# A decoder step whose MLP's first product is made of seven block products for eight, with its activations through DRAM

## The chip, the cores and the metric

The program runs on one core of one Trainium2 chip. The metric is device time in microseconds (us), the median of several runs. A profiled execution gives the trace that all rows below come from.

## The reference, cut to what matters

One step of a decoder layer for 1024 prompt tokens and 32 new tokens (8 sequences of 4), 1056 columns of tokens in all. Attention, a short convolution and their merge come first and are not touched. The change is in the last part:

```
def merge_and_mlp(x, a, c, ga, gb, w_nsa_out, w_conv_out, w_o, g_mlp, w_up, w_down):
    m = jax.nn.sigmoid(ga) * (a @ w_nsa_out) + jax.nn.sigmoid(gb) * (c @ w_conv_out)
    x = x + m @ w_o
    h = rms_norm(x, g_mlp)
    return x + jnp.square(jax.nn.relu(h @ w_up)) @ w_down
```

`h` is 1056 tokens by 1024 features, `w_up` is 1024 x 4096, `w_down` 4096 x 1024, all float32. A final RMSNorm follows.

## The kernel before, in words

Every float32 product is made of three matmuls: an operand is split into a high part (a cast to the type `F32R`) and a low part (what is left), and `mm3` (lines 211 to 214) adds high by high, high by low and low by high. So each line of a product shows up three times in the profile, as L212, L213 and L214. The high part of a weight is cast on ACT, its low part subtracted on POOL (`wsplit`, lines 228 to 236, and `load_down`, lines 1414 to 1424).

**w_o** (lines 1329 to 1359) runs over two halves of 512 output columns, and in each over nine tiles of tokens (eight of 128, one of 32), tokens in rows. In the second half each tile is added to the residual, stored to DRAM (`x2_d`), normalised (ACT squares, POOL takes the root, DVE scales) and transposed on TensorE (`transpose_split`, lines 199 to 209) into `h2h` and `h2l`, high and low parts with features in rows: 8 tiles k of 128 features by 1056 tokens.

**The MLP** (lines 1386 to 1430) goes in eight blocks of four tiles of 128 features of the 4096. In a block the up products come first: for each of the four tiles, three PSUM banks of 384, 384 and 288 token columns (`BANKS`), each summed over 8 k; then ACT's relu, DVE's square, ACT's cast and DVE's low part give `uh` and `ul`, in five buffers. Then the down products of the block: for each of 8 tiles of output features and each of the three banks, four k by three matmuls, added on DVE to `acc`. The up products of the first two tiles (`NU0 = 2`, lines 1361 to 1376) use room that w_o leaves and stand ahead of the blocks:

```
            for c0, c1 in BANKS:
                s = slice(c0, c1)
                po = gemm_T(wu, (h2h, h2l), KT, c0, c1, "up") if f0 >= NU0 * 128 else po0.pop(0)
                r = lp.tile([128, 384], F32, name="r", tag="r")[:, :c1 - c0]
                S.activation(r, po, AF.Relu)
                V.tensor_mul(r, r, r)
                S.copy(uh[:, s], r)
                V.tensor_sub(ul[:, s], r, f32(uh[:, s]))
```

**The end** (from line 1432): the last block's down products come in two groups of columns (`LASTB`, 640 to 1056 and 256 to 640), with the transposes back, the residual and the final norm of each group's tokens behind it; the first 256 tokens come last, with tokens in rows.

**The order of work.** The program says what is done on which engine. Each engine takes its instructions in one order, which a planner sets for the whole program by simulated times; so an engine's order need not be that of the lines. All loads and stores but the gathers are issued by SP, in one queue. A pool of SBUF or PSUM that opens where another closed waits, tile by tile, for the readers of what lay there.

## Time and profile before

| | us |
|---|---|
| median of 3 runs | 2036.77 |
| the runs | 2036.88, 2036.77, 2031.64 |
| the profiled execution, first to last instruction (span) | 2030.1 |
| TensorE busy in it | 1995.6 |
| DVE, ACT, POOL busy | 885.3, 684.3, 602.8 |

Of the profiled execution the trace has the span alone; between it and the median lie 6.7 us. Busy times are sums over the span; a matmul's duration in the trace includes its way through the array, so consecutive matmuls overlap, and what a matmul costs in a row of them is the distance of the starts. PE is TensorE's matmuls, PEld its weight loads, DVE VectorE, ACT ScalarE, POOL GpSimd, SP the engine that issues DMAs.

### The profile page before, as it was taken

How to read it: one execution, taken by the hardware profiler on the slowest of the kernel's cores; microseconds unless marked ns; L12 is line 12 of the kernel's file. 1: busy time of each engine (PE TensorE's matmuls, PEld its weight loads, DVE VectorE, ACT ScalarE, POOL GpSimd, SP SyncE). 2: the span in 40 equal slices, each digit the busy share in tenths (PEclk: the TensorE clock that was granted, in tenths of full speed). 3: DMA queues.
4: the chain of work that ended last, by engine and by line, in shares of the span. 5: the costliest groups of instructions: out<-in, count | busy, mean ns of one | idle time of the engine just before them, and what ended most of it. 6: DMA issues, size and time to landing. Idle time of an engine off the chain costs nothing.

```text
span 2030.1 us, 32304 instructions
## 1 busy us (share of the span) xinstructions
PE 1995.6 (98%) x12644; PEld 1865.3 (92%) x12644; DVE 885.3 (44%) x1930; ACT 684.3 (34%) x1606; POOL 602.8 (30%) x725
## 2 busy tenths in 40 slices
PE   9999999999999999899999899999999999999998
PEld 7999999999998898778788888999999999999998
DVE  5323242445447666464432624534242333333334
ACT  5113224555556566343221303413121222213123
POOL 3121223443344444432332501422122212221203
PEclk9999999999999999999999999999999999999999
DMA  6365226222247311564453534311111111111113
GB/s 209 125 158 132 83 63 168 71 67 65 67 121 246 127 50 48 176 205 156 139 158 132 185 126 139 105 53 42 42 52 42 49 46 47 37 53 41 42 65 117
DMA packets 215463, 205.67 MB, mean 101 GB/s; under 512 B 16213, under 2 KB 185318, under 8 KB 213264
## 3 DMA queue, kind: packets, MB, share of 16 engines
q1 hardware_dynamic: 208400, 170.06, 28.0%
q0 software_dynamic: 6912, 33.56, 4.9%
q8 instruction: 99, 1.62, 0.3%
q14 instruction: 52, 0.43, 0.1%
HBM read 158.95 MB, written 44.63 MB: 100 GB/s over the span
## 4 chain that ended last, share of the span: by engine, by line
PE 78%; DMA 2%; DVE 1%; ACT 1%; issue 0%; POOL 0%; SPq 0%; DVEq 0%; POOLq 0%; ACTq 0%
PE up L214 6%; PE up L212 6%; PE up L213 6%; PE dn L212 6%; PE dn L213 6%; PE dn L214 6%; PE PT L874 3%; PE hid L212 3%; PE ga L213 3%; PE hid L213 3%; PE ga L212 3%; PE ga L214 3%; PE hid L214 3%; PE pv L881 2%; PE pv L880 2%; PE sl L1127 2%
## 5 line engine op out<-in xcount | busy, mean ns | idle before, releaser
L235 POOL TENSOR_TENSOR wlu<-wru,whu 128x1024 fp32r<-128x1024 f32 x62 | 149.3, 2409 | 483.4 <-ACT whu L234 483.4
L213 PE MATMUL dn<-ul,whd 128*128 128x384 f32 (+2 forms) x736 | 239.1, 325 | 0.0
L214 PE MATMUL dn<-uh,wld 128*128 128x384 f32 (+2 forms) x736 | 239.1, 325 | 0.0
L212 PE MATMUL dn<-uh,whd 128*128 128x384 f32 (+2 forms) x736 | 238.3, 326 | 0.0
L212 PE MATMUL up<-h2h,whu 128*128 128x384 f32 (+1 forms) x720 | 232.9, 323 | 0.0
L214 PE MATMUL up<-h2h,wlu 128*128 128x384 f32 x720 | 232.8, 324 | 0.0
L213 PE MATMUL up<-h2l,whu 128*128 128x384 f32 (+1 forms) x720 | 232.5, 323 | 0.0
L800 POOL TENSOR_SCALAR P<-P,st,gates 128x256 f32<-128x256 f32 (+4 forms) x272 | 150.7, 571 | 123.1 <-DVE st L796 94.3
L1400 DVE TENSOR_TENSOR r<-r 128x384 f32<-128x384 f32 (+1 forms) x96 | 108.2, 1128 | 180.2 <-ACT r L1399 178.3
L1412 DVE TENSOR_TENSOR acc<-dn,acc 128x384 f32<-128x384 f32 (+1 forms) x160 | 84.3, 528 | 195.1 <-PE dn L214 195.1
L1423 POOL TENSOR_TENSOR wld<-wrd,whd 128x512 fp32r<-128x512 f32 x64 | 83.8, 1311 | 248.4 <-ACT whd L1422 248.4
L212 PE MATMUL hid<-cth,w1h 128*128 128x254 f32 x512 | 148.5, 290 | 5.7 <-ACT cth L509 5.6
L213 PE MATMUL hid<-ctl,w1h 128*128 128x254 f32 x512 | 149.6, 292 | 0.0
L214 PE MATMUL hid<-cth,w1l 128*128 128x254 f32 x512 | 145.7, 285 | 0.0
L214 PEld LDWEIGHTS dn<-uh,wld 128*128 128x128 f32 x736 | 138.4, 188 | 0.0
L213 PEld LDWEIGHTS dn<-ul,whd 128*128 128x128 f32 x736 | 138.4, 188 | 0.0
L212 PEld LDWEIGHTS dn<-uh,whd 128*128 128x128 f32 x736 | 137.9, 188 | 0.1
L213 PEld LDWEIGHTS up<-h2l,whu 128*128 128x128 f32 x720 | 135.8, 189 | 0.0
L212 PEld LDWEIGHTS up<-h2h,whu 128*128 128x128 f32 x720 | 135.4, 188 | 0.0
L214 PEld LDWEIGHTS up<-h2h,wlu 128*128 128x128 f32 x720 | 135.3, 188 | 0.0
L1422 ACT CAST whd<-wrd 128x512 fp32r<-128x512 f32 x64 | 39.8, 621 | 265.3 <-PE dn L213 263.6
L212 PE MATMUL ga<-hTh,whu 128*128 128x384 f32 (+1 forms) x384 | 127.8, 333 | 0.0
(410 smaller groups left out, 4927.0 us busy)
## 6 DMA issues: line engine op xcount, KB each, us to landing
wru<-in_w_in SPq DMA_DIRECT2D x32, 512.0 KB
wrd<-in_w_down SPq DMA_DIRECT2D x64, 256.0 KB
wru<-in_w_up SPq DMA_DIRECT2D x30, 512.0 KB
tb<-tb_d SPq DMA_DIRECT2D x8, 528.0 KB
cg_d<-tb SPq DMA_DIRECT2D x8, 528.0 KB
ta<-ta_d SPq DMA_DIRECT2D x8, 528.0 KB
cg<-cg_d SPq DMA_DIRECT2D x8, 528.0 KB
w1r<-in_cmp_w_k SPq DMA_DIRECT2D x16, 256.0 KB
```

Of the source, the lines that this page charges most:

```text
L212: PE.matmul(out, wh, ah, start=first, stop=False)
L213: PE.matmul(out, wh, al, start=False, stop=False)
L214: PE.matmul(out, wl, ah, start=False, stop=last)
L235: (leng or P.tensor_sub)(l, raw, f32(h))
L800: P.tensor_scalar(p, p, self.st[:, br, 3, g:g + 1], gates[:, self.qi, 3 * hg + br:3 * hg + br + 1], op0=OP.mult, op1=OP.mult)
L874: PE.transpose(pt[:n, g * 128:(g + 1) * 128], pg[g], ident)
L880: PE.matmul(self.o, w, hi[:n], start=first and i == 0, stop=False)
L881: PE.matmul(self.o, w, lo[:n], start=False, stop=last and i == len(tiles) - 1)
L1127: PE.matmul(pl[l][rows[j], :], qb[b], kt, start=True, stop=True)
L1400: V.tensor_mul(r, r, r)
L1412: V.tensor_add(acc[:, j, s], po, acc[:, j, s])
L1423: P.tensor_sub(l, raw, f32(h))
```

## The change

The 1024 features of `h` are taken as two halves, the 1056 tokens as two halves of 528 (each with 512 prompt tokens and 16 new ones, which changes the order of the columns), and the 4096 features of the MLP as 16 pairs of tiles (p and p + 16). Of such a 2 x 2 x 2 product, seven block products of [512 x 128] by [512 x 528] are made for eight, from sums and differences of the blocks of `w_up` (s1 to s4, on DVE, anew for each pair) and of `h` (t1 to t4, once, on POOL and DVE); sums of the products give the four results. The operands that are made of `h` are split into high and low parts in a stage after w_o; the first block product's two operands (`hA`) are split tile by tile as before. In w_o's second half the 32 new tokens come fifth, not last. `relu(x)` times `x` is one DVE operation; its result is stored to DRAM (`u_d`) and loaded again by the down products, which become a stage of their own and keep their blocks of four. PSUM is four double banks during the up products. The last block's groups of columns are 264, 264 and 272 wide.

```diff
+HC = T // 2
...
-NU0 = 2
...
-LASTB = [(640, T), (256, 640)]
+LASTB = [(HC, HC + 264, (4, 5)), (HC + 264, T, (6, 7)), (256, HC, (2, 3, 8))]
+TORDER = [(0, 1, 2, 3, 4, 5, 6, 7, 8), (0, 1, 2, 3, 8, 4, 5, 6, 7)]
+NP0 = 2
+WUB = 7
...
+    u_d = dr.tile([32, 128, 2, HC], F32, name="u_d")
...
     h2p = open_pool("h2", "left")
-    h2h = h2p.tile([128, KT, T], F32R, name="h2h")
-    h2l = h2p.tile([128, KT, T], F32R, name="h2l")
+    hA = [[h2p.tile([128, 4, HC], F32R, name=f"hA{q}{x}") for x in "hl"] for q in range(2)]
+    h2r = [[[h2p.tile([128, HC], F32, name="h2r", tag="h2r", bufs=16) for _ in range(4)] for _ in range(2)] for _ in range(2)]
+    (r11, r12), (r21, r22) = h2r
     fp = open_pool("F", "left", bufs=2)
     g2 = fp.tile([128, D], F32, name="g2", bufs=1)
     DMA.dma_start(g2, g_mlp.to_broadcast([128, D]))
+    def columns(tt):
+        if tt < 8:
+            return [(tt // 4, slice(tt % 4 * 128, tt % 4 * 128 + 128), slice(0, 128))]
+        return [(h, slice(512, HC), slice(16 * h, 16 * h + 16)) for h in range(2)]
+    def transpose_h2(xn, m, tt):
+        for q in range(2):
+            pt = ps("tp", "xT")
+            pv = pt.rearrange("p (k t) -> p k t", k=4)
+            for i in range(4):
+                k = 4 * q + i
+                PE.transpose(pv[:, i, :m], xn[:m, k * 128:(k + 1) * 128], ident[:m, :m])
+            for half, c, s in columns(tt):
+                for k in range(4):
+                    S.copy(h2r[q][half][k][:, c], pv[:, k, s])
+                if half == 0:
+                    h = hA[q][0][:, :, c]
+                    V.tensor_copy(h, pv[:, :, s])
+                    V.tensor_sub(hA[q][1][:, :, c], pv[:, :, s], f32(h))
+        c = columns(tt)[-1][1]
+        if tt >= 4:
+            for k in range(4):
+                P.tensor_sub(r11[k][:, c], r12[k][:, c], r11[k][:, c])
+                P.tensor_sub(r12[k][:, c], r22[k][:, c], r12[k][:, c])
     for half in range(2):
         hs = slice(half * 512, half * 512 + 512)
         if half:
             wo = load_wo(1)
-        for tt in range(9):
+        for tt in TORDER[half]:
...
-                transpose_split(xn, m, h2h, h2l, tt * 128)
-    po0 = []
-    for j in range(NU0):
-        wu0 = []
+                transpose_h2(xn, m, tt)
+    early_w = []
+    for p in range(NP0):
         for q in range(2):
             raw, h, l = (wop.tile([128, 512], dt, name="wo" + n, tag="wo" + n, bufs=b).rearrange("p (k c) -> p k c", k=4)
                          for n, dt, b in (("r", F32, 2), ("h", F32R, WOB), ("l", F32R, WOB)))
-            DMA.dma_start(raw, w_up[0, q * 512:(q + 1) * 512, j * 128:(j + 1) * 128].rearrange("(k p) c -> p k c", p=128))
+            DMA.dma_start(raw, w_up[0, q * 512:(q + 1) * 512, p * 128:(p + 1) * 128].rearrange("(k p) c -> p k c", p=128))
             S.copy(h, raw)
             V.tensor_sub(l, raw, f32(h))
-            wu0 += [(h[:, k], l[:, k]) for k in range(4)]
-        for c0, c1 in BANKS:
-            po = ps("gx", "up")[:, :c1 - c0]
-            for k in range(KT):
-                mm3(po, *wu0[k], h2h[:, k, c0:c1], h2l[:, k, c0:c1], k == 0, k == KT - 1)
-            po0.append(po)
-    close("F", "wo", "m")
+            early_w.append((h, l))
+    open_psum(c=4)
+    def product(w, h):
+        c = bank["p"].tile([128, 2, 512], F32, name="c", tag="c", bufs=4)[:, :, :HC // 2]
+        for k in range(4):
+            for i in range(2):
+                s = slice(i * HC // 2, (i + 1) * HC // 2)
+                low = h[1][k] if isinstance(h[1], list) else h[1][:, k]
+                mm3(c[:, i], w[0][:, k], w[1][:, k], h[0][:, k, s], low[:, s], k == 0, k == 3)
+        return c
+    close("F")
+    qp = open_pool("q", "left")
+    def part(tag, bufs=1):
+        return qp.tile([128, 2, HC // 2], F32, name=tag, tag=tag, bufs=bufs)
+    def first_two(w11, w12):
+        p1 = part("p1", NP0)
+        S.copy(p1, product(w11, hA[0]))
+        x = part("x", 3)
+        V.tensor_add(x, product(w12, hA[1]), p1)
+        return p1, x
+    begun = [first_two(*early_w[2 * p:2 * p + 2]) for p in range(NP0)]
+    close("wo", "m")
+    hbp = open_pool("hB", "right")
+    t2 = [hbp.tile([128, HC], F32, name="t2", tag="t2", bufs=4) for _ in range(4)]
+    for k in range(4):
+        V.tensor_sub(t2[k], r22[k], r11[k])
+        V.tensor_sub(r21[k], r21[k], t2[k])
+    hB = {}
+    for n, raw, low, pool, tag in (("t2", t2, V, hbp, "l2"), ("t3", r12, P, hbp, "t2"), ("t1", r11, V, h2p, "h2r"),
+                                   ("t4", r21, P, h2p, "h2r"), ("b22", r22, V, h2p, "h2r")):
+        h = hbp.tile([128, 4, HC], F32R, name="hB" + n)
+        l = [pool.tile([128, HC], F32R, name=tag, tag=tag, bufs=16 if tag == "h2r" else 4) for _ in range(4)]
+        for k in range(4):
+            S.copy(h[:, k], raw[k])
+            low.tensor_sub(l[k], raw[k], f32(h[:, k]))
+        hB[n] = (h, l)
+    wp = open_pool("w", "right", bufs=2)
+    def halves(raw):
+        h, l = (wp.tile([128, 4, 128], F32R, name="wu" + x, tag="wu" + x, bufs=WUB) for x in "hl")
+        S.copy(h, raw)
+        P.tensor_sub(l, raw, f32(h))
+        return h, l
+    def put(f, half, x):
+        u = part("u", 4)
+        V.scalar_tensor_tensor(u, x, 0.0, x, op0=OP.max, op1=OP.mult)
+        DMA.dma_start(u_d[f, :, half], u.rearrange("p i c -> p (i c)"))
+    for p in range(16):
+        raws = []
+        for f in (p, p + 16):
+            raw = wp.tile([128, KT, 128], F32, name="wru", tag="wru", bufs=4)
+            DMA.dma_start(raw, w_up[0, :, f * 128:(f + 1) * 128].rearrange("(k p) c -> p k c", p=128))
+            raws += [raw[:, :4], raw[:, 4:]]
+        w11, w12, w21, w22 = raws
+        s1, s2, s3, s4 = (wp.tile([128, 4, 128], F32, name=f"s{i}", tag=f"s{i}", bufs=1) for i in range(4))
+        V.tensor_add(s1, w21, w22)
+        V.tensor_sub(s2, s1, w11)
+        V.tensor_sub(s3, w11, w21)
+        V.tensor_sub(s4, w12, s2)
+        p1, x = begun[p] if p < NP0 else first_two(halves(w11), halves(w12))
+        put(p, 0, x)
+        u2 = part("u2")
+        V.tensor_add(u2, product(halves(s2), hB["t2"]), p1)
+        u3 = part("u3")
+        V.tensor_add(u3, product(halves(s3), hB["t3"]), u2)
+        c = product(halves(s1), hB["t1"])
+        x = part("x", 3)
+        V.tensor_add(x, c, u3)
+        V.tensor_add(u2, c, u2)
+        put(p + 16, 1, x)
+        x = part("x", 3)
+        V.tensor_add(x, product(halves(w22), hB["t4"]), u3)
+        put(p + 16, 0, x)
+        x = part("x", 3)
+        V.tensor_add(x, product(halves(s4), hB["b22"]), u2)
+        put(p, 1, x)
+    close("w", "hB", "q", "h2")
+    open_psum(**GEMM)
     accp = open_pool("acc", "right")
     acc = accp.tile([128, KT, T], F32, name="acc")
     lp = open_pool("mlp", "right", bufs=2)
     for blk in range(NBLK):
         us = []
         for j in range(NU):
-            f0 = (blk * NU + j) * 128
-            if f0 >= NU0 * 128:
-                wu = wsplit(wp, w_up[0, :, f0:f0 + 128], KT, 128, "u")
+            raw = lp.tile([128, T], F32, name="ur", tag="ur", bufs=3)
+            DMA.dma_start(raw, u_d[blk * NU + j].rearrange("p h c -> p (h c)"))
             uh = lp.tile([128, T], F32R, name="uh", tag="uh", bufs=NU + 1)
             ul = lp.tile([128, T], F32R, name="ul", tag="ul", bufs=NU + 1)
             us.append((uh, ul))
-            for c0, c1 in BANKS:
-                s = slice(c0, c1)
-                po = gemm_T(wu, (h2h, h2l), KT, c0, c1, "up") if f0 >= NU0 * 128 else po0.pop(0)
-                r = lp.tile([128, 384], F32, name="r", tag="r")[:, :c1 - c0]
-                S.activation(r, po, AF.Relu)
-                V.tensor_mul(r, r, r)
-                S.copy(uh[:, s], r)
-                V.tensor_sub(ul[:, s], r, f32(uh[:, s]))
+            S.copy(uh, raw)
+            V.tensor_sub(ul, raw, f32(uh))
...
+    def residual(tt):
+        m = 128 if tt < 8 else 32
+        t0 = tt * 128
         xt = op.tile([128, D], F32, name="x2", tag="x2", bufs=6)
         DMA.dma_start(xt[:m], x2_d[t0:t0 + m, :])
+        if tt == 8:
+            new = op.tile([128, KT, 2, 16], F32, name="new", bufs=1)
+            V.tensor_copy(new, acc.rearrange("p k (h c) -> p k h c", h=2)[:, :, :, 512:])
+            new = new.rearrange("p k h c -> p k (h c)")
+        else:
+            new = acc[:, :, tt // 4 * HC + tt % 4 * 128:][:, :, :128]
         for q in range(2):
             pt = ps(YT[q], "yT")
             h = slice(q * 512, q * 512 + 512)
             for i in range(4):
-                PE.transpose(pt[:m, i * 128:(i + 1) * 128], acc[:, 4 * q + i, t0:t0 + m], ident)
+                PE.transpose(pt[:m, i * 128:(i + 1) * 128], new[:, 4 * q + i], ident)
             V.tensor_add(xt[:m, h], pt[:m], xt[:m, h])
         return xt
...
+    early = [residual(tt) for tt in (0, 1)]
+    for c0, c1, tts in LASTB:
         for j in range(8):
             down(j, lambda k: [z[:, k % 2, j % 2 * 128:j % 2 * 128 + 128] for z in wds[k // 2 * 4 + j // 2]], c0, c1)
-        for t0 in range(c0, c1, 128):
-            m = min(128, T - t0)
-            xt = residual(t0, m)
+        for tt in tts:
+            t0, m = tt * 128, 128 if tt < 8 else 32
+            xt = residual(tt)
...
```

## Rows read from the trace of the kernel before

**Rows 1.** The page's first part: busy time, share and instructions of each engine.

```profile
PE 1995.6 (98%) x12644; PEld 1865.3 (92%) x12644; DVE 885.3 (44%) x1930; ACT 684.3 (34%) x1606; POOL 602.8 (30%) x725
```

**Rows 2.** The page's chain that ended last: by engine, then by line.

```profile
PE 78%; DMA 2%; DVE 1%; ACT 1%; issue 0%; POOL 0%; SPq 0%; DVEq 0%; POOLq 0%; ACTq 0%
PE up L214 6%; PE up L212 6%; PE up L213 6%; PE dn L212 6%; PE dn L213 6%; PE dn L214 6%; PE PT L874 3%; PE hid L212 3%; PE ga L213 3%; PE hid L213 3%; PE ga L212 3%; PE ga L214 3%; PE hid L214 3%; PE pv L881 2%; PE pv L880 2%; PE sl L1127 2%
```

**Rows 3.** Busy us (count) by engine, clock, DMA share, GB/s, 1500 to 1600.

```profile
1500.00:1600.00 100.00, 100.00 (x625) 100.00 (x624) 35.15 (x51) 22.53 (x40) 21.26 (x13) 1.00 0.15 43
```

**Rows 4.** The chain in order of time: start, us, what; at block starts.

```profile
1417.41 0.32 PE dn L212 x2
...
1510.21 0.31 PE dn L212 x2
```

**Rows 5.** TensorE in order of time, an up stage: start, duration, operation.

```profile
1499.72 0.34 PE L214 MATMUL up<-h2h,wlu 128*128 128x384 f32 x1
...
1501.47 0.30 PE L212 MATMUL up<-h2h,whu 128*128 128x288 f32 x1
...
1504.65 0.34 PE L212 MATMUL dn<-uh,whd 128*128 128x384 f32 x1
```

**Rows 6.** TensorE in order of time, the tail's matmuls of 256 columns.

```profile
2012.85 0.28 PE L212 MATMUL dn<-whd,uh 128*128 128x256 f32 x1
...
2015.96 0.29 PE L214 MATMUL dn<-whd,ul 128*128 128x256 f32 x1
```

**Rows 7.** Groups by line and shape: count, busy us, mean ns, idle before.

```profile
L1423 POOL TENSOR_TENSOR wld<-wrd,whd 128x512 fp32r<-128x512 f32 x64 | 83.8, 1311 | 248.4 <-ACT whd L1422 248.4
...
L1422 ACT CAST whd<-wrd 128x512 fp32r<-128x512 f32 x64 | 39.8, 621 | 265.3 <-PE dn L213 263.6 <-DMA wrd<-in_w_down 1.7
```

**Rows 8.** DVE in order of time, two low parts of 512 columns.

```profile
1266.11 1.29 DVE L1370 TENSOR_TENSOR wol<-wor,woh 128x512 fp32r<-128x512 f32 x2
```

**Rows 9.** Busy time by engine, granted clock and DMA, 2005 to 2010.

```profile
2005.00:2010.00 5.00, 5.00 (x35) 4.97 (x34) 1.96 (x5) 2.46 (x5) 0.59 (x2) 1.00 0.61 241
```

**Rows 10.** TensorE in order of time, the last product of w_o.

```profile
1268.36 0.47 PE L226 MATMUL wo<-wol,m 128*64 128x512 f32 x1
```

**Rows 11.** ACT in order of time, the last cast of the last tile's transposes.

```profile
1281.04 0.27 ACT L208 CAST h2h<-xT 128x128 fp32r<-128x128 f32 x1 [0.33 <-PE xT L206]
```

**Rows 12.** The page's groups: POOL's low part of 1024 columns.

```profile
L235 POOL TENSOR_TENSOR wlu<-wru,whu 128x1024 fp32r<-128x1024 f32 x62 | 149.3, 2409 | 483.4 <-ACT whu L234 483.4
```

**Rows 13.** POOL in order of time, around the first blocks.

```profile
1289.17 5.11 POOL L235 TENSOR_TENSOR wlu<-wru,whu 128x1024 fp32r<-128x1024 f32 x2 [12.17 <-ACT whu L234]
```

**Rows 14.** DVE in order of time, the same stretch.

```profile
1281.73 1.03 DVE L1400 TENSOR_TENSOR r<-r 128x384 f32<-128x384 f32 x2
...
1289.52 2.50 DVE L1400 TENSOR_TENSOR r<-r 128x384 f32<-128x384 f32 x1 [0.87 <-ACT r L1399]
1291.94 4.24 DVE L1402 TENSOR_TENSOR ul<-r,uh 128x288 fp32r<-128x288 f32 x2
```

**Rows 15.** SP's DMA issues in order of time, before the last block.

```profile
1968.79 0.35 SPq L1436 DMA_DIRECT2D gf<-in_g_final  x1
```

**Rows 16.** ACT in order of time, the operation that waited for that load.

```profile
1973.13 1.06 ACT L1438 ACTIVATE gf<-gf 128x1024 f32<-128x1024 f32 x1 [2.91 <-DMA gf<-in_g_final]
```

**Rows 17.** TensorE in order of time, up products at the start of the blocks.

```profile
1296.34 0.34 PE L213 MATMUL up<-h2l,whu 128*128 128x384 f32 x1
1296.52 0.30 PE L212 MATMUL up<-h2h,whu 128*128 128x288 f32 x1
```

**Rows 18.** TensorE in order of time, the merge, idle time in brackets.

```profile
1120.97 0.53 PE L212 MATMUL na<-aTh,whd 128*128 128x288 f32 x2 [1.18 <-ACT aTh L1274]
```

**Rows 19.** Busy time by engine, granted clock and DMA, around that wait.

```profile
1120.00:1125.00 5.00, 3.59 (x18) 3.35 (x19) 2.86 (x7) 1.39 (x3) 1.39 (x2) 0.81 0.00 0
1125.00:1130.00 5.00, 5.00 (x28) 5.00 (x28) 3.31 (x6) 1.92 (x4) 2.60 (x3) 0.85 0.56 188
```

**Rows 20.** POOL in order of time, the sample rows' last scaling.

```profile
2010.10 2.38 POOL L1483 TENSOR_TENSOR yt<-yt,gf 32x1024 f32<-32x1024 f32 x1 [1.21 <-ACT yt L1482]
```

More of the change, by code (lines that the diff above doesn't have):

```diff
@@ L1430, in tile_hybrid_step @@
                     down(j, lambda k: (wd[0][:, k], wd[1][:, k]), c0, c1)
-    close("h2")
     op = open_pool("out", "left", bufs=3)
@@ L1439, in tile_hybrid_step @@
     Q4 = [slice(q * 256, q * 256 + 256) for q in range(4)]
-    def residual(t0, m):
+    def residual(tt):
+        m = 128 if tt < 8 else 32
+        t0 = tt * 128
         xt = op.tile([128, D], F32, name="x2", tag="x2", bufs=6)
         DMA.dma_start(xt[:m], x2_d[t0:t0 + m, :])
+        if tt == 8:
[4 more added lines that the diff above has]
+            new = acc[:, :, tt // 4 * HC + tt % 4 * 128:][:, :, :128]
         for q in range(2):
@@ L1463, in factor @@
         return rs
-    early = [residual(t0, 128) for t0 in (0, 128)]
-    for c0, c1 in LASTB:
+    early = [residual(tt) for tt in (0, 1)]
+    for c0, c1, tts in LASTB:
         for j in range(8):
             down(j, lambda k: [z[:, k % 2, j % 2 * 128:j % 2 * 128 + 128] for z in wds[k // 2 * 4 + j // 2]], c0, c1)
-        for t0 in range(c0, c1, 128):
-            m = min(128, T - t0)
-            xt = residual(t0, m)
+        for tt in tts:
+            t0, m = tt * 128, 128 if tt < 8 else 32
+            xt = residual(tt)
             yt = op.tile([128, D], F32, name="yt", tag="yt")
```

## Prediction

> **What bounds the kernel now.** I read the page's busy shares first: TensorE works 98% of the span, no other engine half of it [rows 1]. The chain that ended last says the same and says where: its largest lines are the products named up (by w_up) and dn (by w_down), and DMA has 2% of it [rows 2]. Then the table by stretches: from 1500 to 1600 us TensorE is busy for all 100 us at the full granted clock (1.00, the 2.4 GHz level), with DVE at 35%, ACT at 23%, POOL at 21%, 43 GB/s of DMA [rows 3]. So in the MLP only TensorE's own work counts, as long as nothing makes it wait. The chain in order of time shows the length of one block (four tiles of 128 features up, then down): the same down products come 92.80 us apart [rows 4].
>
> **The pace of one matmul.** Durations overlap, so I take starts. Ten matmuls of 384 columns lie between 1499.72 and 1501.47 (0.175 us each), 24 of 288 between 1501.47 and 1504.65 (0.1325) [rows 5]. A block has 192 times two of 384 and one of 288: 192 x 0.4825 = 92.6 us, the measured 92.8; half of it, 46.4, is the up products, and over eight blocks they cost 371.2 us. In the tail there are matmuls of 256 columns, each with weights of its own: 26 starts in 3.11 us, 0.1196 each [rows 6]. Between 256 and 288 the line gives 0.1228 for 264; I take 0.123.
>
> **The change, part by part.**
>
> *Up products.* Seven products for each of 16 pairs of feature tiles, each of 4 k by 2 token quarters by 3 matmuls of 264 columns: 16 x 7 x 24 = 2688 matmuls (2304 before), 2688 x 0.123 = 330.6 us. That removes 40.6 us of the path. Bounds: at 256's pace 321.5 (49.7 gained), at 288's 356.2 (15.0 gained). Columns alone fall by an eighth (46.4 us); 384 more starts give some 6 back.
>
> *Inside the loop over pairs* (20.7 us of TensorE each): POOL has seven low parts of 128x512 at 1.31 us [rows 7], 9.2 us; ACT seven casts at 0.62 [rows 7] and one way out of PSUM, 5 us; DVE four sums of weights and seven additions out of PSUM at about 0.65 (1.29 for two of 512 columns [rows 8]) and four squares, about 10 us. Each fits, even if one after the other; PSUM holds four products, and weights run up to seven halves ahead. I cost it at nothing; the cover is the 20.7 us, and if it is gone, a pair loses what is over. Four stores (1.06 MB a pair) and 1 MB of weights are 100 GB/s, against 241 in a stretch of the tail [rows 9]. On SP a store waits for DVE with the next weights behind it; these are wanted a pair later.
>
> *Hand-over from w_o to the pairs.* Before, the last w_o matmul ends at 1268.83 [rows 10] and ACT's last cast of the last tile's transposes at 1281.31 [rows 11]: a lag of 12.5 us, covered by up products of the tokens already there. Now the last tile is a full one, and the first two products of two pairs need only the first half of the tokens: 96 matmuls, 11.8 us, and 0.9 us of transposes. After that everything needs differences that hang on the last tile. POOL: 8 of 128 columns, 8 low parts of 528, 5 of weights; by 1.31 us at 512 columns [rows 7] and 2.41 at 1024 [rows 12] that is 8 x 0.49 + 8 x 1.34 + 5 x 1.31 = 21.2 us. DVE: 20 of 528 columns and 4 of 512, 15.8 us. If both run side by side from 10.5 us after w_o (POOL's first differences start before the lag is over), POOL ends at 31.7; unhindered, TensorE would have done the first pair's last product at 0.9 + 11.8 + 14.8 = 27.5, so some 5 us late. If they take turns, they end at 47.5, 20 us late. The trace shows turns: while POOL's two low parts of 1024 ran (5.11 us from 1289.17), a DVE product of 384 columns took 2.50 us and the next two operations, of 288, took 4.24 together, where two of 384 took 1.03 a little earlier with POOL idle [rows 13, 14]. I take 9 us: the sums and halves of the weights need no tile and can be over by then, and only a part of the ops meet.
>
> The Trainium skill, SBUF — State Buffer, section Who interferes with whom, says that a DVE instruction with two SBUF inputs contends with a GpSimd one that reads SBUF, and that the second to issue is blocked until the first ends. By that rule every one of those 24 DVE operations can wait for a POOL one, and the hand-over would cost the 20 us, not 9; the trace agrees on single operations [rows 13, 14], and how many meet no run shows yet.
>
> *Hand-over from the pairs to w_down.* All up products are now over before the first down product. By the sizes of the pools in the order in which they open, the first buffer for w_down lies on the halves of s4, which the very last up product reads, and the four u tiles of a block come from DRAM through three buffers. A load of 512 KB took 4.3 us from its issue (1968.79) to the operation that waited for it (1973.13) [rows 15, 16]; with the cast of 0.62 TensorE can start some 5 us after its last product, with POOL's 1.31 on top for the low part. Two u tiles can be loaded before that. The order of TensorE's queue is planned, and a planner that knows of a late low part puts other banks' high products first: at 1296.34 and 1296.52 two matmuls by the high weights stand together, for another bank, without the third [rows 17]. On SP a u load that waits for its buffer has w_down's next loads behind it, and these TensorE. Bounds 0 and 9 us (no overlap of four conversions); I take 5.
>
> *Block boundaries.* Five u buffers serve blocks of four. Before, 11.6 us of up products lay between two u tiles; now the second to fourth of a block can be cast only when the last group of the block before has read them, 1.2, 0.8 and 0.4 us ahead of its end. One cast of 1056 columns is about 1.1 us, three low parts on DVE about 1.3 each (by 0.65 for 512): the fourth u is there some 3.8 us after the boundary. Six free PSUM banks hold 2.9 us of work for each k, so with the groups interleaved nearly nothing is lost; in order, the first group (2.1 us) ends 2.2 us late, up to 6 with POOL's low parts in DVE's way. Behind a u cast that waits on ACT stand w_down's casts, and behind them POOL and TensorE. Seven boundaries: 0 to 42 us; I take 0.7 each, 4.9.
>
> *Clock.* A short wait costs more than itself: TensorE waited 1.2 us ahead of 1120.97 [rows 18], and the granted clock is 0.81 and 0.85 in the two stretches of 5 us from 1120, a fall to the 1.2 GHz level for a part of them [rows 19]: (0.19 + 0.15) x 5 = 1.7 us lost. Two hand-overs: 3.4.
>
> *End.* The last groups are 264, 264 and 272 columns wide for 416 and 384: 96 x (0.123 + 0.123 + 0.1265 - 0.190 - 0.1755) = +0.7 us. The sample rows now come in the last group, with POOL's 2.38 us [rows 20] between other POOL work of the tail, and one DVE scaling less: bounds -1.3 and 2.5, I take 1.2. In w_o, more copies (eight of 128 columns at 0.27 [rows 11]) fit in ACT's slack: nothing.
>
> **Sum.** -40.6 + 9 + 5 + 4.9 + 3.4 + 0.7 + 1.2 = -16.4. The profiled span is 2030.1 us; 6.7 us lie between it and the median of the runs, 2036.8. So 2013.7 of span, and 2020 us.
>
> **Rivals.**
> 1. *The hand-overs are covered after all.* For it: the planner interleaves [rows 17], and waits of TensorE before are rare. Then 4 us in all are lost beside the end's 1.9: 2036.8 - 40.6 + 5.9 = 2002.
> 2. *The lock sets the first hand-over.* DVE and POOL take turns for the whole preparation: 20 instead of 9, and 4 more at the second: 2035, no change to be told. For it [rows 13, 14]; against it, that ACT's casts between the operations space them out.
> 3. *Block boundaries, the side of slower.* Each of the seven costs 4 us (between 2.2 and 6) and a fall of the clock (1.5), because DVE's low part is planned without POOL in the way and TensorE's queue keeps its order: 38.5 instead of 4.9, 2054. It decides from 3.0 us a boundary on (the 16.4 us gained, plus 4.9, over seven). For it: five buffers for four, and [rows 14]; against it, six banks of work.
> 4. *It doesn't do what it says:* the pace at 264 columns is that of 288. Then 15.0 are gained, not 40.6: 2046. Against it, [rows 6] with fresh weights for each matmul.
>
> **Chances.** Forecast 0.60 (2006 to 2032), rival 1 0.14, rival 2 0.12, rival 3 0.10, rival 4 0.04. 0.3% is 6 us, about what a measurement of this kernel can tell from none. Faster (under 2030.7): 0.6 less a small upper part, 0.57, 0.14 of rival 1 and 0.03 of rival 2: 0.74. Same: that part and 0.08 of rival 2: 0.11. Slower: rivals 3 and 4 and the rest of 2: 0.15. The range takes in rivals 1 and 2: 2000 to 2037.
>
> **What would show it.** Starts of matmuls in the pairs 0.123 us apart, and a pair 20.7 us; gaps of TensorE of about 9 us after w_o (waiting for DVE or POOL) and 5 before the first down product (waiting for w_down's cast or u); a block of down products of 46.4 us, a boundary gap under 1. Wrong would be: a pair over 21.5 us, so that an engine behind TensorE sets the loop; blocks over 49 us; or a first hand-over over 15.

## The result: slower by half a per cent, and the profile after

The changed kernel takes 2046.14 us (median; 2043.53 to 2047.89), the kernel before 2036.63 beside it: a ratio of 1.0054, 95% interval 1.0038 to 1.0069. Forecast were 2020 us, 2000 to 2037. The profiled execution after is 2047.57 us with a span of 2045.8; that of before was the shortest of its runs (2031.64, span 2030.1), so the two traces lie 15.7 us apart, the medians 9.5.

TensorE is busy for less of the span than before [rows 1], and the chain has DMA at 6% where it had 2% [rows 2]. First the page's lines of busy time and chain:

```profile
PE 1963.6 (96%) x13124; PEld 1832.7 (90%) x13124; DVE 999.4 (49%) x2041; ACT 687.8 (34%) x1622; POOL 707.3 (35%) x851
...
PE 87%; DMA 6%; DVE 3%; ACT 2%; issue 1%; SPq 1%; POOL 1%; DVEq 0%; POOLq 0%; ACTq 0%
```

Then the table by stretches (busy us and count by engine, granted clock, DMA share, GB/s), which answers to [rows 3]:

```profile
1250.00:1300.00 50.00, 35.73 (x182) 30.71 (x181) 25.02 (x35) 23.41 (x89) 24.27 (x51) 0.76 0.19 65
1300.00:1350.00 50.00, 34.62 (x262) 34.37 (x262) 42.58 (x45) 13.71 (x25) 34.88 (x23) 0.83 0.44 123
1350.00:1600.00 250.00, 250.00 (x2063) 250.00 (x2062) 160.46 (x187) 59.44 (x98) 112.47 (x86) 1.00 0.34 104
1600.00:1650.00 50.00, 39.11 (x323) 38.90 (x321) 23.87 (x27) 9.72 (x13) 9.49 (x13) 0.92 0.32 121
1650.00:1700.00 50.00, 41.89 (x249) 41.89 (x250) 13.52 (x22) 10.74 (x16) 18.43 (x14) 0.88 0.53 173
1700.00:1950.00 250.00, 250.00 (x1557) 250.00 (x1556) 101.91 (x154) 51.31 (x68) 56.88 (x43) 1.00 0.31 97
```

The loop over pairs (1350 to 1600) and the down blocks (from 1700) are full, at a clock of 1.00. All that is missing is missing around the two hand-overs, where the clock too is partly at its lower level. TensorE's waits name both (us in total, times, longest; 1260 to 1700):

```profile
PE dn L216 <- ACT whd L1533: 19.0, 1, 19.0
PE c L216 <- ACT wuh L1455: 15.4, 1, 15.4
PE xT L1349 <- DVE xn L1393: 8.0, 3, 6.2
PE xT L1349 <- ACT h2r L1352: 6.3, 1, 6.3
```

**How long each stage is.** The same DVE addition of two pairs in a row shows the length of a pair, 20.39 us (DVE in order of time):

```profile
1607.09 0.71 DVE L1480 TENSOR_TENSOR u<-c,p 128x528 f32<-128x528 f32 x1 [0.41 <-PE c L218]
...
1627.48 0.71 DVE L1480 TENSOR_TENSOR u<-c,p 128x528 f32<-128x528 f32 x1 [1.38 <-PE c L218]
```

Sixteen pairs are 326.2 us, 45.0 less than the 371.2 of the up products before. But from w_o's last product to the last up product TensorE needs 1269.56 to 1638.95, 369.4 us: 43.2 of them go into the first hand-over. They are 29.7 of waits (14.3 ahead of and between the transposes, 15.4 behind the begun products), 3.5 of transposes at the full pace, and some 10, by an estimate from the rest, that the lower clock costs. The second takes 19.2 more, to 1658.11, and the first products of w_down run at the lower clock for 3.7 us. The landmarks (TensorE in order of time, idle time in brackets; the gap of 15.38 us stands behind the begun pairs' products):

```profile
1269.56 0.40 PE L218 MATMUL wo<-woh,mTl 128*128 128x512 f32 x1
...
1290.68 1.94 PE L1349 MATMUL xT<-cst,xn 128*128 128x128 f32 x8 [1.60 <-DVE xn L1393]
1292.27 0.57 PE L216 MATMUL c<-hA0h,woh 128*128 128x264 f32 x1
...
1296.38 0.42 PE L216 MATMUL c<-hA0h,woh 128*128 128x264 f32 x1
...
1296.91 0.29 PE L216 MATMUL c<-hA0h,woh 128*128 128x264 f32 x1
1297.04 0.29 PE L217 MATMUL c<-hA0l,woh 128*128 128x264 f32 x1
...
1321.52 0.59 PE L216 MATMUL c<-hBt,wuh 128*128 128x264 f32 x1 [15.38 <-ACT wuh L1455]
```

Before, the last cast of the transposes ended 12.5 us behind w_o's last product [rows 10, 11], and the up products ran on in between. Now it ends 23.5 us behind (ACT's copies until 1293.43); the transposes themselves begin 21.1 us behind (1290.68). The begun products, whose operands had been ready since 1276.7, stand behind them in TensorE's queue and start at half the pace (0.22 us each until 1296.6, after that 0.12; the granted clock is 0.58 from 1269 to 1293). The first products behind the gap run at that pace again until 1327.3.

**What was late in the first hand-over.** GpSimd, in order of time: the scale of a tile (`rs`, line 201) and its first half (`ss`, line 200) stand among the pieces of the differences (lines 1361 and 1362), which the kernel writes per tile. Of the last two tiles ACT has the sum of squares at 1280.6 and 1284.3, GpSimd the scale at 1285.5 and 1289.0:

```profile
1282.19 0.19 POOL L200 TENSOR_SCALAR ss<-ss 128x1 f32<-128x1 f32 x1
1282.46 0.87 POOL L1362 TENSOR_TENSOR h2r<-h2r 128x128 f32<-128x128 f32 x2
1283.29 1.69 POOL L1361 TENSOR_TENSOR h2r<-h2r 128x128 f32<-128x128 f32 x4
1284.94 0.55 POOL L201 TENSOR_TENSOR rs<-ss,nhalf 128x1 f32<-128x1 f32 x1
...
1295.89 3.59 POOL L1362 TENSOR_TENSOR h2r<-h2r 128x128 f32<-128x128 f32 x4
```

And DVE: it waits for those scales and pieces, then runs its own operations beside GpSimd's, many at 1.8 us for the 0.7 of others of that size, and the sums of the weights, behind all of them, wait 1.04 us for their load:

```profile
1285.52 1.47 DVE L1393 SCALAR_TENSOR_TENSOR xn<-x,rs,g 128x1024 f32<-128x1024 f32 x1 [2.48 <-POOL rs L201]
...
1293.78 1.83 DVE L1439 TENSOR_TENSOR t<-h2r 128x528 f32<-128x528 f32 x2 [3.25 <-POOL h2r L1361]
...
1303.13 1.82 DVE L1449 TENSOR_TENSOR h2r<-h2r,hBt 128x528 fp32r<-128x528 f32 x1 [1.23 <-POOL t L1449]
1304.87 0.70 DVE L1449 TENSOR_TENSOR l<-t,hBt 128x528 fp32r<-128x528 f32 x1
...
1315.99 1.83 DVE L1449 TENSOR_TENSOR h2r<-h2r,hBb 128x528 fp32r<-128x528 f32 x2
1318.86 0.69 DVE L1473 TENSOR_TENSOR s<-wru 128x512 f32<-128x512 f32 x1 [1.04 <-DMA wru<-in_w_up]
```

The load in turn had been issued late: SP has a store of `u_d` (1312.01), which waits for DVE, ahead of the weights of the next pairs.

What TensorE waits for behind the begun products is the cast of s2, and so those sums (ACT in order of time). The other operand, t2, was there long before: its last low part ended at 1308.5.

```profile
1320.85 1.66 ACT L1455 CAST wuh<-s 128x512 fp32r<-128x512 f32 x3 [15.76 <-DVE s L1474]
```

**What was late in the second.** SP's issues in order of time:

```profile
1638.12 0.38 SPq L1546 DMA_DIRECT2D gf<-in_g_final  x1
1638.61 1.34 SPq L1508 DMA_DIRECT2D ur<-u_d  x3
1640.62 0.32 SPq L1463 DMA_DIRECT2D u_d<-u  x1
1641.00 4.76 SPq L1556 DMA_DIRECT2D x<-x_d  x6
1646.82 0.32 SPq L1508 DMA_DIRECT2D ur<-u_d  x1
1647.50 1.58 SPq L1530 DMA_DIRECT2D wrd<-in_w_down  x2
```

The loads of the residual rows and of the last scale, not wanted for 300 us, stand between the u tiles and w_down's first weights. On ACT w_down's first cast stands behind the cast of the fourth u tile, whose load took 9.7 us from its issue (ACT in order of time):

```profile
1656.47 1.07 ACT L1512 CAST uh<-ur 128x1056 fp32r<-128x1056 f32 x1 [8.57 <-DMA ur<-u_d]
1657.44 0.61 ACT L1533 CAST whd<-wrd 128x512 fp32r<-128x512 f32 x1
```

Before, the residual rows and the scale were issued from 1968.79 on [rows 15], when the last up products had freed their room; after the change that room is free at the end of the pairs.

### The profile page after: what moved, and what is told of

It is laid out like the page before. It is cut to its first block, busy times and chain, and to the rows that moved or that the text cites. A ratio compares the mean times of both kernels' runs of the same rounds, so it can differ in the third digit from the quotient of the medians.

```text
span 2045.8 us, 34190 instructions
## 1 busy us (share of the span) xinstructions
PE 1963.6 (96%) x13124; PEld 1832.7 (90%) x13124; DVE 999.4 (49%) x2041; ACT 687.8 (34%) x1622; POOL 707.3 (35%) x851
## 4 chain that ended last, share of the span: by engine, by line
PE 87%; DMA 6%; DVE 3%; ACT 2%; issue 1%; SPq 1%; POOL 1%; DVEq 0%; POOLq 0%; ACTq 0%
PE dn L216 6%; PE dn L217 6%; PE dn L218 6%; PE c L216 5%; PE c L217 5%; PE c L218 5%; PE PT L878 3%; PE ga L217 3%; PE ga L216 3%; PE ga L218 3%; PE hid L217 3%; PE hid L216 3%; PE hid L218 3%; PE pv L885 2%; PE pv L884 2%; PE sl L1131 2%
## 5 line engine op out<-in xcount | busy, mean ns | idle before, releaser
L216 PE MATMUL dn<-uh,whd 128*128 128x384 f32 (+3 forms) x768 | 240.5, 321 | 19.0 <-ACT whd L1533 19.0
L217 PE MATMUL dn<-ul,whd 128*128 128x384 f32 (+3 forms) x768 | 244.4, 319 | 0.0
L218 PE MATMUL dn<-uh,wld 128*128 128x384 f32 (+3 forms) x768 | 243.2, 318 | 0.0
L1523 DVE TENSOR_TENSOR acc<-dn,acc 128x384 f32<-128x384 f32 (+2 forms) x168 | 84.2, 511 | 174.6 <-PE dn L218 174.3
L216 PE MATMUL c<-hBt,wuh 128*128 128x264 f32 x512 | 146.9, 287 | 15.4 <-ACT wuh L1455 15.4
L216 PEld LDWEIGHTS dn<-uh,whd 128*128 128x128 f32 x768 | 144.2, 189 | 19.2 <-ACT whd L1533 19.2
L218 PE MATMUL c<-hBt,wul 128*128 128x264 f32 x512 | 145.9, 286 | 0.0
L882 DVE TENSOR_TENSOR ptl<-PT,pth 128x512 fp32r<-128x512 f32 (+1 forms) x148 | 99.5, 686 | 64.4 <-ACT pth L881 64.0
L217 PE MATMUL ga<-hTl,whu 128*128 128x384 f32 (+1 forms) x384 | 126.3, 329 | 0.0
L218 PE MATMUL ga<-hTh,wlu 128*128 128x384 f32 (+1 forms) x384 | 125.9, 328 | 0.0
L216 PEld LDWEIGHTS c<-hBt,wuh 128*128 128x128 f32 x512 | 97.6, 191 | 15.6 <-ACT wuh L1455 15.6
```

The source lines that it names most:

```text
L216: PE.matmul(out, wh, ah, start=first, stop=False)
L217: PE.matmul(out, wh, al, start=False, stop=False)
L218: PE.matmul(out, wl, ah, start=False, stop=last)
L882: V.tensor_sub(lo[:n], pt[:n], f32(hi[:n]))
L1523: V.tensor_add(acc[:, j, s], po, acc[:, j, s])
```

## The experiments

Ratios are to the kernel before, with their 95% intervals; the changed kernel has 1.0054, and 0.0010 is 2 us. "Gap 1" is TensorE's wait behind the begun pairs, "gap 2" that ahead of w_down. "Start" is how long behind w_o's last product the first product after the begun pairs starts: w_o's last product itself comes anywhere from 1268.0 to 1278.4 us in these traces, because the stages ahead of w_o vary (w_o itself takes 104.5 to 105.0 us in all of them), so times of two traces are compared from there. Two traces with the same code up to there agree within 0.8 us (52.0 and 51.4, 45.8 twice, 38.1 and 38.9).

| run | ratio | start | gap 1 | gap 2 |
|---|---|---|---|---|
| the change | 1.0054 [1.0038, 1.0069] | 52.0 | 15.4 | 19.0 |
| three buffers | 1.0044 [1.0029, 1.0058] | 47.6 | 16.2 | 19.3 |
| weights first | 1.0041 [1.0025, 1.0057] | 47.9 | 14.3 | 19.3 |
| hold residual | 1.0019 [1.0010, 1.0029] | 51.4 | 16.2 | 10.9 |
| these three | 0.9999 [0.9989, 1.0009] | 45.8 | 14.4 | 12.2 |
| + no GpSimd | 0.9954 [0.9936, 0.9971] | 35.9 | 10.4 | 11.1 |
| + pieces only | 0.9951 [0.9937, 0.9966] | 38.8 | 12.4 | 11.0 |
| + lows only | 0.9982 [0.9968, 0.9995] | 42.8 | 11.6 | 11.0 |
| the change, no GpSimd | 1.0003 [0.9986, 1.0020] | 41.0 | 11.1 | 19.3 |
| three + early room | 0.9987 [0.9975, 1.0000] | 45.8 | 14.7 | 7.9 |
| three + three begun | 0.9977 [0.9968, 0.9987] | 47.4 | 9.7 | 12.0 |
| all | 0.9931 [0.9914, 0.9949] | 38.1 | 5.9 | 7.7 |
| all, ACT issues | 0.9903 [0.9886, 0.9921] | 38.9 | 5.9 | 4.7 |
| all, four begun | 0.9935 [0.9917, 0.9953] | 46.2 | 6.5 | 7.9 |
| all, both | 0.9904 [0.9885, 0.9923] | 46.0 | 6.7 | 4.7 |
| all, without the first two edits | 0.9957 [0.9943, 0.9971] | 45.7 | 8.3 | 8.1 |

### The loads' order and buffers

**Three buffers.** In w_o's second half the additions come 9.3 us apart (1257.13, 1266.41) for TensorE's 6.42 before: with two buffers, the load of a tile waits for the scaling of the one before.

```diff
-                xf = fp.tile([128, D], F32, name="x2", tag="x2")
+                xf = fp.tile([128, D], F32, name="x2", tag="x2", bufs=3)
...
-                xt = fp.tile([128, 512], F32, name="xo", tag="xo")
+                xt = fp.tile([128, D], F32, name="xo", tag="x2", bufs=3)[:, :512]
```

> Change against the changed kernel: the tile of x that w_o's result is added to gets three buffers instead of two, in the same room (the smaller tile for the other half takes the same buffers). Theory A (the ring load of x -> add -> scaling -> buffer free sets w_o's second half at about 9.2 us for a tile): the adds come about 6.5 to 7.5 us apart, the four transposes that were outstanding behind w_o's last product are fewer, the begun products start 6 to 10 us earlier, and the time falls by 5 to 10 us, to 2036 to 2041. Rival B (VectorE and GpSimd, slowed by each other, set the first hand-over whatever the loads do): the transposes come earlier, but the low parts of the second half of the differences end where they ended, TensorE's 15 us wait grows by what the transposes gave, and the time stays within 2 us of 2046.

2043.64 us. Some transposes moved in among w_o's products; the last ones begin 16.6 us behind w_o's last product for 21.1, and the start comes 4.4 us earlier. That is less than theory A's 6 to 10 and more than rival B's nothing. Theory A's 5 to 10 us of time are not there; the measured 2 lie near rival B's, though the interval tells them neither from none nor from 4.

**Weights first.**

```diff
+        if after is not None:
+            V.tensor_copy(u[:, 0, :1], f32(after[:, 0, :1]))
         V.scalar_tensor_tensor(u, x, 0.0, x, op0=OP.max, op1=OP.mult)
...
-        put(p, 0, x)
+        hs2 = halves(s2)
+        put(p, 0, x, hs2[0] if p < NP0 else None)
```

> Change against the changed kernel: in the first two pairs VectorE also copies one column of the next pair's weights into the tile that is about to be filled, so that on SP the store of the first products stands behind the weights' loads instead of ahead of them. Theory A (the 15.4 us wait of TensorE at about 1306 us is the wait of the weights' loads behind that store): the wait shrinks to what the low parts of the differences leave (the last that the next products need end about 1309 to 1318 us), so by 4 to 10 us; time 2036 to 2042. Rival B (the low parts set it): the wait keeps 12 us or more, time 2043 to 2047.

2044.16 us, gap 1 at 14.3: B by the wait and by the time, though the start is 4.0 us earlier. The loads went first (from 1305.79), and the sums of the weights now waited for no load, but still stood behind all of DVE's low parts (they begin at 1317.52).

**Hold the residual rows.**

```diff
+    V.tensor_copy(gf[:, :1], acc[:, 7, :1])
     DMA.dma_start(gf, g_fin.to_broadcast([128, D]))
...
+        V.tensor_copy(xt[:m, :1], acc[:m, 7, :1])
         DMA.dma_start(xt[:m], x2_d[t0:t0 + m, :])
```

> Change against the changed kernel: the loads of the residual rows (six, 3 MB) and of the last scale, which are issued at 1638 to 1646 us between the last up product's store and w_down's first weights, are held until w_down's sixth block is done, by a one-column copy from that block's sum. Theory A (their 3 MB ahead in the queues make the second hand-over 19 us): TensorE's wait before the first product of w_down falls to 7 to 10 us, the time by 9 to 12 us, to 2034 to 2037. Rival C (the way of u through DRAM and the clock alone make it): the wait keeps 15 us or more, and the time stays above 2042. Either way nothing is lost at the end, where the kernel before had these loads as late.

2039.60 us: 7 us of the expected 9 to 12. Gap 2 falls from 19.0 to 10.9 us (TensorE in order of time), so theory A holds here, for a part. In the 11 us that are left the fourth u tile waits for one of three buffers: its load is issued when DVE's first low part is done (1641.68). And w_down's first cast still stands behind its cast on ACT (1645.53 and 1646.51).

```profile
1647.17 0.69 PE L216 MATMUL dn<-uh,whd 128*128 128x384 f32 x1 [10.92 <-ACT whd L1533]
```

**The three together.**

> The three edits together. Theory A: the gains add but for what they share in the first hand-over (the transposes and the wait of the pair weights): 20 to 30 us less than the changed kernel, 2016 to 2026, and so 10 to 20 us below the kernel before. Rival B: only the held loads count, 2034 to 2037, no faster than the kernel before.

2034.25 us, level with the kernel before and in rival B's range: the small gains add (0.0010, 0.0013, 0.0035 make 0.0058; measured 0.0055), but the 20 to 30 us that theory A promised are not there. The first hand-over has another master.

### GpSimd's part of the first hand-over

**No GpSimd.** On top of the three edits, the pieces and the low parts of t3 and t4 go to DVE:

```diff
-                P.tensor_sub(r11[k][:, c], r12[k][:, c], r11[k][:, c])
-                P.tensor_sub(r12[k][:, c], r22[k][:, c], r12[k][:, c])
+                V.tensor_sub(r11[k][:, c], r12[k][:, c], r11[k][:, c])
+                V.tensor_sub(r12[k][:, c], r22[k][:, c], r12[k][:, c])
...
-    for n, raw, low, pool, tag in (("t2", t2, V, hbp, "l2"), ("t3", r12, P, hbp, "t2"), ("t1", r11, V, h2p, "h2r"),
-                                   ("t4", r21, P, h2p, "h2r"), ("b22", r22, V, h2p, "h2r")):
+    for n, raw, low, pool, tag in (("t2", t2, V, hbp, "l2"), ("t3", r12, V, hbp, "t2"), ("t1", r11, V, h2p, "h2r"),
+                                   ("t4", r21, V, h2p, "h2r"), ("b22", r22, V, h2p, "h2r")):
```

> On top of the three edits together (2034.25 us): GpSimd's part of the first hand-over is given to VectorE: the 64 pieces of the differences r (in the tile loop) and the low parts of t3 and t4. In the trace of the three edits two tiles' scales (1286.6 and 1290.0 us, GpSimd) stand behind those pieces in GpSimd's queue, and VectorE's operations take 1.75 us beside GpSimd's for 0.68 alone. Theory B (the two engines slow each other, and the pieces hold back the scales): the last transposes come 4 to 8 us earlier, VectorE's operations take 0.6 to 0.7 us again, and the first product of the first pair after the begun ones starts 6 to 12 us earlier; time 2022 to 2029. Theory D (the weights' loads, issued at 1307 us when the begun products have freed their room, set that start): the start follows the loads and moves by the transposes' gain alone, time 2028 to 2031. Theory E (VectorE is the bound, and GpSimd's help is worth more than the slowing costs): no gain or a loss, 2033 to 2038.

(The pieces are 40, five tiles with eight each, not 64.) 2024.56 us, 9 to 10 less: theory B (the last transposes come 5.4 us earlier, the start 9.9). DVE does everything and is done sooner, since with GpSimd idle each operation of 528 columns takes 0.62 us of it (DVE in order of time):

```profile
1295.60 2.56 DVE L1440 TENSOR_TENSOR h2r<-h2r,t 128x528 f32<-128x528 f32 x4
1298.07 1.32 DVE L1449 TENSOR_TENSOR l<-t,hBt 128x528 fp32r<-128x528 f32 x2
...
1309.20 2.56 DVE L1449 TENSOR_TENSOR h2r<-h2r,hBb 128x528 fp32r<-128x528 f32 x4
1311.68 0.69 DVE L1475 TENSOR_TENSOR s<-wru 128x512 f32<-128x512 f32 x1
```

**Which of the two.** The same edit in halves: the first two lines alone, the last two alone.

> On top of the first three edits together (its ratio to the kernel before is 0.9999; with all of GpSimd's part given away 0.9954): only the 64 pieces of the differences r go to VectorE, the low parts of t3 and t4 stay on GpSimd. If the pieces are what cost (they hold the scales in GpSimd's queue and slow VectorE until 1301 us), this alone gives three quarters or more of those 0.45%, a ratio of 0.995 to 0.9965, and the lag from w_o's last product to the last transposes falls from 16.7 us to about 13. If it is the low parts, it gives a quarter or less: 0.999 to 1.000.

> The counterpart: only the low parts of t3 and t4 go to VectorE. If the slowing of VectorE in the low parts (1.75 us each beside GpSimd's for 0.70 alone, 1303 to 1318 us) is what sets the start: a ratio of 0.996 to 0.998 with TensorE's wait shorter by 4 to 7 us; if the pieces are: 0.9985 to 1.001, since eight operations of 0.62 us more stand on VectorE, and as much slowing goes.

By the times the pieces give all of it (2025.97 us), the low parts by themselves less than half (2031.84, a ratio between the two expected ranges); the intervals are some 3 us wide to either side. The traces tell more: of the 9.9 us of the start the pieces alone give 7.0, the low parts alone 3.0. With the pieces gone, a scale follows its first half at once (GpSimd in order of time), and the last transposes begin 11.4 us behind w_o's last product, for 16.6 in the run of the three edits, which is 5.2 of the 7.0:

```profile
1278.89 0.19 POOL L200 TENSOR_SCALAR ss<-ss 128x1 f32<-128x1 f32 x1 [3.21 <-ACT xn L199]
1279.16 0.55 POOL L201 TENSOR_TENSOR rs<-ss,nhalf 128x1 f32<-128x1 f32 x1
```

The low parts do slow DVE there (1.83 us for one of 528 columns at 1295.17). It costs nothing that the times can tell; in the traces the start comes 2.9 us later than with GpSimd out of it altogether. No run leaves the pieces on GpSimd but behind the scales, so how much of their 7.0 us is their place in the queue and how much the slowing of the two engines is not separated; that the scales follow at once speaks for the queue in the 5.2.

**The same edit in the changed kernel as it is.**

> GpSimd's part given to VectorE in the changed kernel as it is (two buffers for the tile of x, the first stores ahead of the weights' loads, the residual rows' loads early). If GpSimd's part alone set the first hand-over: 9 to 12 us below the changed kernel, a ratio to the kernel before of 0.999 to 1.001 (the changed kernel's is 1.0054). If the loads' order and buffers are late by nearly as much, as the run without the two first edits suggests: 4 to 8 us below, 1.0015 to 1.0035.

2037.38 us, 9 to 10 us below the change, the start 11.0 earlier: GpSimd's part costs as much without the loads' edits as with them.

### The cover, the room and the queue

**Three begun pairs** (`NP0 = 3` for 2, on top of the three edits).

> On top of the three edits together: three pairs' first products are begun before the preparation instead of two, 6.3 us more of work for TensorE in the gap of 14.4 us. Theory B (the preparation on VectorE and GpSimd sets the start of the next product): the start stays where it is within 1 us (it was at 1321.4 us) and the gap is filled by 6 us, time 2027 to 2030. Theory D (the weights' loads, which wait for the room of the begun products' weights, set it): the loads are issued some 6 us later, the start moves with them, and the time stays within 2 us of 2034.

2029.92 us: 4.5 us gained, between the two. The start is at 47.4 us for 45.8, so it moves by 1.6 us and the rest is filled.

**Early room.** The pools behind the pairs change places, so that u and w_down's weights lie on what the last pair reads first (on top of the three edits):

```diff
-    accp = open_pool("acc", "right")
-    acc = accp.tile([128, KT, T], F32, name="acc")
-    lp = open_pool("mlp", "right", bufs=2)
+    lp = open_pool("mlp", "left", bufs=2)
     wp = open_pool("w", "right", bufs=2)
+    accp = open_pool("acc", "right")
+    acc = accp.tile([128, KT, T], F32, name="acc")
```

> On top of the three edits together: the tiles of u and of w_down's weights are laid over what the last pair reads first (the high and low parts of the blocks of h in the first two products; t2's and t3's), the sum over what it reads last, so that the loads need not wait for the last product. Theory F (what is left of the second hand-over, 12.2 us of wait, is the loads of u and of w_down from the last product on, because their room is not free before): the wait falls to 1 to 4 us, no half clock follows it, and the time falls by 8 to 12 us, to 2022 to 2026. Rival: the loads then run beside the last pair's, or the casts of u by ACT and VectorE set the start, and the wait keeps 8 us or more; 2031 to 2035.

2033.60 us, gap 2 at 7.9: only 2.4 us, as the rival had it. The room was there, the order was not: SP (in order of time) has the loads behind stores of `u_d` that wait for DVE's products of the last pair.

```profile
1604.52 31.32 SPq L1465 DMA_DIRECT2D u_d<-u  x7
1635.94 1.36 SPq L1511 DMA_DIRECT2D ur<-u_d  x3
1637.39 0.38 SPq L1533 DMA_DIRECT2D wrd<-in_w_down  x1
```

**All of it** (the three edits, no GpSimd, early room, three begun).

> All of it together: the three edits, no GpSimd in the preparation, the early room, three begun pairs. If B and F hold, the gains add (6 to 12, 8 to 12, and what is left of the first gap, 3 to 6): 2007 to 2018 us, clearly below the kernel before (2035.7). If D holds and F too: 2020 to 2026. If neither: 2033 to 2036.

2019.14 us, 14 us below the kernel before, just above the range for B and F; by the ratios the gains overlap by some 2 us, which is within the noise.

**ACT issues** the first block's u loads and first two weights:

```diff
-            DMA.dma_start(raw, u_d[blk * NU + j]
+            (S if blk == 0 else DMA).dma_start(raw, u_d[blk * NU + j]
...
-            DMA.dma_start(raw, w_dn[0, f0:f0 + kt * 128
+            (S if blk == 0 and c < 2 else DMA).dma_start(raw, w_dn[0, f0:f0 + kt * 128
```

> On top of all together (2019.1 us): the loads of the first down block's u tiles and first two weight tiles are issued by ACT instead of SP. In the trace of all together SP's queue has them behind a store of u that waits for VectorE's product of the last pair (issues from 1636 us where the room was free some us before), and TensorE waits 7.7 us. Theory G (SP's order sets what is left of the second hand-over): the loads go 5 us or more earlier, the wait falls to 0 to 3 us, time 2012 to 2015. Rival (the room or the casts set it): the wait keeps 5 us or more, time 2017 to 2020.

2016.89 us, the fastest version: 20 us below the kernel before, 30 below the change. Wait and time lie between theory G's and the rival's. The loads now go 17 us ahead of the last up product (ACT in order of time). What is left of gap 2, 4.7 us, is ACT's own queue: the load of the fourth u tile (1628.67) waits for a buffer, which DVE's first low part frees, and behind its issue stand the third cast of u and w_down's casts:

```profile
1608.60 1.34 ACTq L1511 DMA_DIRECT2D ur<-u_d  x3
1613.50 4.18 ACTq L1533 DMA_DIRECT2D wrd<-in_w_down  x2
...
1628.67 0.34 ACTq L1511 DMA_DIRECT2D ur<-u_d  x1
1629.05 1.07 ACT L1515 CAST uh<-ur 128x1056 fp32r<-128x1056 f32 x1 [9.21 <-DVE ul L1516]
1630.03 1.13 ACT L1536 CAST whd<-wrd 128x512 fp32r<-128x512 f32 x2
```

**Four begun pairs** (`NP0 = 4`, with one u buffer less and one x buffer more), alone and with ACT's issues.

> On top of all together: four pairs begun instead of three (with one u buffer less and one x buffer more, for the room). TensorE waits 5.9 us there in the trace of all together, and VectorE's sums of the weights start with the loads' landing (1304.69 us, a wait of 0.31 us for the load). If the loads' room sets the start (theory D now, with the preparation out of the way), the start moves by part of the 6.3 us that the fourth pair takes and the gain is 1 to 4 us, 2015 to 2018; if VectorE's low parts set it (theory B), the gap closes, 2013 to 2015.

> Four begun pairs and ACT's issues together: the two places are 300 us apart and should add: 2007 to 2012 us if both gain, 2012 to 2016 if one does.

2022.30 and 2017.53 us: nothing gained, both above all that was expected. DVE's first sum of weights waits for its load, 3.11 us, where with three begun pairs it waited 0.31 (DVE in order of time, in both kernels):

```profile
1311.53 0.69 DVE L1475 TENSOR_TENSOR s<-wru 128x512 f32<-128x512 f32 x1 [3.11 <-DMA wru<-in_w_up]
```

```profile
1304.69 0.69 DVE L1475 TENSOR_TENSOR s<-wru 128x512 f32<-128x512 f32 x1 [0.31 <-DMA wru<-in_w_up]
```

That fits theory D: the weights' room is the begun pairs', and a fourth pair gives it back later (SP issues the second load at 1307.51, right behind the last begun product at 1307.32). The smaller u ring was not tried by itself.

**Without the first two edits.**

> All together without the first two edits (two buffers for the tile of x again, the first stores ahead of the weights' loads again). With GpSimd out of the preparation the loads may now be what is late, where they gave little before (2.5 and 2.0 us): theory A in this form expects 5 us or more lost, 2024 to 2030. If three buffers and the order of SP don't matter here either, 2019 to 2023.

2028.43 us, in theory A's range. By the ratios the three buffers and SP's order are worth 5 us here and 4 ahead (1.0019 to 0.9999), by the start 7.5 and 5.6. So they add to what GpSimd's part gives; whether they are worth more once that is out of the way, the intervals don't tell.

## Why the prediction was wrong, step by step

- **Up products, -40.6: right.** Starts 0.121 us apart, a pair 20.39 us for 20.7; the term is -45.0. Rival 4 is out. Inside the loop nothing waits, as costed.
- **Hand-over from w_o to the pairs, +9 (bounds 5 and 20): this step failed.** It took 43.2 us, of which the kernel before had 4.2 (3.1 of transposes, 1.1 of waits): +39, outside both bounds. The price per operation was right where an engine ran alone, and so was the lock [rows 13, 14]. Two things that the sum took as given were not so.
  - *When the preparation starts.* The sum has it run from 10.5 us behind w_o, as "POOL's first differences start before the lag is over"; DVE's part starts 23.8 us behind (1293.78). Those differences stand in GpSimd's queue ahead of the scales of the next tiles, so they lengthen the lag itself, together with the ring of x, of which the text priced only ACT's copies (23.5 us for the 12.5 taken; the loads' edits give 4.5 of it back, the pieces 5.2 more).
  - *What runs beside it.* The sum has TensorE do the whole first pair, 14.8 us, while POOL still works, as the sums of the weights "can be over by then". In the trace the first of these products starts when all of the preparation is over: DVE's part takes 24.0 us for 15.8, and the four sums stand behind it. It is so in every run of the table, and no run moves them, so what this order costs by itself is not shown; in the change their load comes no sooner either, since "wanted a pair later" is true of every pair but the first.
  - By the times, taking the pieces away gives 8 to 10 us, the two loads, costed at nothing, 4 to 5, and a third begun pair 4.5.
- **The lock, rival 2 (20 us for 9).** The Trainium skill, SBUF — State Buffer, section Who interferes with whom, says that a DVE instruction with two SBUF inputs contends with a GpSimd one that reads SBUF; the traces agree on the operation, 1.83 us for 0.62 beside GpSimd. But the low parts, the larger operations, are the smaller part of it: left on GpSimd once the pieces are gone, they cost nothing that the times tell (0.9951 against 0.9954) and 2.9 us of the start. That DVE's part ends 47.9 us behind w_o, where rival 2 has 47.5, is chance: it starts 13 us later and lasts 24 us for 37.
- **Hand-over to w_down, +5 (bounds 0 and 9): failed too,** 21 us with the clock's part. The load's price of 4.3 us did not hold behind the residual rows (9.7 us for the fourth u tile; 3.9 with the rows held). And "two u tiles can be loaded before that" asks for room and for a place in SP's queue: with the room alone the u loads went no earlier, with room and ACT's queue 17 us ahead of the last up product. By the times holding the residual rows gives 7 us, room and ACT's queue 8 more. That other loads would move into freed room was not considered.
- **Block boundaries, +4.9: too high.** No wait of TensorE behind 1700; from 1708.83 to 1940.38 five blocks take 46.3 us each. Rival 3 is out; six products by high parts stand together at a block's start (1708.83), and no cast made TensorE wait.
- **Clock, +3.4:** the falls came and cost more than 1.7 us each, some 10 us (an estimate) in the first hand-over with its longer waits and 1.9 behind the second. They are counted above.
- **The base.** The 6.7 us between span and median were those of a profiled run at the lower end of its spread; between the medians, 6 us of the traces' difference of 15.7 are not there.
- By stages, in the traces: the up products with their hand-over 6.0 us shorter (369.4 for 371.2 and 4.2; forecast: 30), the second hand-over 19.2 longer, what follows to the last product 1.4 longer (the lower clock's 1.9 in it): 14.6, and w_o ends 1.2 later, which makes the 15.7 but for rounding.
- With the gaps cut to 5.9 and 4.7 the kernel's 2016.89 us lie near the forecast's 2020, and that is luck in part: the first hand-over still takes 23.9 us there, 9 more than forecast with its clock, and the 4.4 us more of the up products and the 4.9 of the block boundaries, which never came, pay for it.

## What to carry to other kernels

When one stage is split in two, cost the hand-over as a chain with every queue in it: list for each in-order queue what stands ahead of the first operation that the next stage needs, the scalings, stores and loads of other stages included, and see what the newly free room lets in there. Work that is "free" because its engine is idle is free only where nothing on the path stands behind it in that engine's queue. And ask of each small operation that was costed as done early where it stands in its queue: here four sums of 0.7 us, behind 24 us of work, were what TensorE waited for.

## What the runs showed of the hardware that was not expected

- GpSimd as a helper of DVE can be worth less than nothing: beside each other a DVE operation of 528 columns takes 1.75 to 1.83 us and GpSimd's about 1.7, two in 1.75 us; DVE alone does one in 0.62, two in 1.24.
- Two operations on one column (a tile's scale, 0.75 us of GpSimd's time) were ready some 4 us late for each of the last two tiles once 40 pieces of 0.2 to 0.9 us shared their queue; with the pieces moved the last transposes began 5.2 us earlier.
